# Down projection of a decoder layer: splitting its f operands one tile at a time, with a smaller first chunk

## The chip, the cores and the metric

The kernel runs on 1 core of one Trainium2 chip. The metric is the device time of one execution in microseconds (us); lower is better. Three runs of the kernel before gave 2714.26 us as their median, 2711.56 us as the fastest and 2715.88 us as the slowest.

## The reference

The program is one layer of an autoregressive decoder with 512 positions and a model width of 2048, in float32: a mixer of two attentions, then a gated feed-forward part with a short causal convolution. The change touches only the end of the feed-forward part:

```python
def conv_ffn(h, w_up, w_conv, b_conv, w_down):
    S = h.shape[1]
    u = h @ w_up
    up = jnp.pad(u, ((0, 0), (CONV_W - 1, 0), (0, 0)))
    conv = b_conv
    for j in range(CONV_W):
        conv = conv + w_conv[j] * up[:, j:j + S]
    gate, val = jnp.split(conv, 2, axis=-1)
    return (jax.nn.silu(gate) * val) @ w_down

x = x + gt_f * conv_ffn(h, w_up[l], w_conv[l], b_conv[l], w_down[l])
```

`f = silu(gate) * val` has 5632 rows (channels) of 512 positions, which are 44 row tiles of 128. The down projection multiplies it with `w_down` (5632 x 2048).

## The kernel before

**Precision.** TensorE multiplies in a shortened float32 format. To keep accuracy, each operand is split into a high part (a copy by ScalarE, line 114) and a low part (the rest, a subtraction by VectorE, line 115), and each product is made of three matmuls (lines 1065 to 1067). Weights are split into three pairs of buffers, `whi` and `wlo`; activations are split into slots.

**Seven products for eight.** `seven` works through a list of `Pair`s. A pair is two output tiles of 128 rows, each 512 positions wide. It is computed by a Strassen-like scheme with seven steps instead of eight quarter products. A step has K products of 128x128 weights with 256 positions, so 3K matmuls. The seven steps use seven operand kinds, in the order `r11`, `t3`, `t2`, `r21`, `t1`, `t4`, `r22`. VectorE also combines the raw weight blocks (line 965, four times a pair), and ScalarE and VectorE take each step's result out of PSUM (lines 969 and 975, or 971 and 977 in the up projection). Weights are prepared two steps ahead of their matmuls (`AHEAD = 2`). The raw weight blocks pass through five buffers, loaded on SP's queue at line 952.

**Up projection.** The up pairs have K = 8. When a pair ends, `ffn_out` convolves its two tiles and makes f, and `f_out` stores f and its differences to scratch memory in DRAM (lines 1373 and 1382, GpSimd's queue).

**Down projection.** The 44 row tiles of f don't fit into the on-chip slots as split operands, so they are worked through in four chunks. `DH` is the number of row-tile pairs in each chunk, which is also K for the steps of its pairs: 6, 6, 5 and 5, that is chunks of 12, 12, 10 and 10 row tiles. A chunk has 8 pairs of output tiles, so 56 steps. The first three chunks add their result to `x1` in DRAM with an accumulating DMA from GpSimd's queue (line 1526); the last chunk loads `x1`, adds it (line 1523) and stores the output (line 1524).

**Making the operands of a chunk.** For each kind of a chunk, `load_set` fetches its half tiles of f from scratch into raw slots with one DMA for each half tile on SP's queue (line 1459), the same queue that loads the weights. `split_set` then turns all raw tiles of that kind into high and low tiles: one ScalarE and one VectorE instruction of 128x512 for each raw tile, three raw tiles a set (the third is half filled where K = 5). A set's high and low tiles stay in their slots until the last pair of the chunk has used this kind. There are 81 slots, handed out from a queue: the slot freed longest ago is taken first. A chunk of 3 raw tiles by 7 kinds holds 42 slots when all of it is split; results on their way to DRAM and the raw tiles use slots too.

**When they are made.** `hook` runs after each step and calls `ahead`, which may split one set and load others if enough slots are free. Far from the end of a chunk a set may be split at every fourth step, and no more than four of seven sets; in the last eight steps of a chunk every step may split one. During the up projection the sets of the first chunk are made under the same rule (50 steps before its end at the earliest), but there the two operands of the up projection hold most slots until its last pair.

A scheduler puts all instructions of each engine into one fixed order, by its own estimate of times and by data dependencies. So where an instruction stands in its engine's queue is known from the built program, and an instruction that waits holds up all that stands behind it in that queue.

Of the kernel before, what the change touches and what calls it, by code (L numbers as in the profile page):

```python
# [19 lines left out]
T = 512  # L20
# [11 lines left out]
def trunk_layer_kernel(  # L32
# [15 lines left out]
    HG=2,  # L48
    AFT=(-1,),
    PEU=((2, 5, 8, 11, 14),) * 2 + ((),) * 6,  # L50
    DH=(6, 6, 5, 5),
):
    nc = tc.nc
    V, A, G, PE, SP = nc.vector, nc.scalar, nc.gpsimd, nc.tensor, nc.sync
# [8 lines left out]
    free = deque(range(n_slots))  # L63
    held = {}

    def get(dt=F32):
        i = free.popleft()
        if cur[i] is None or cur[i].dtype != dt:
            cur[i] = pool.tile([P, T], dt, name=f"slot{i}", tag=f"slot{i}")
        held[id(cur[i])] = i  # L70
        return cur[i]

    def getr():
        return get(F32R)

    def put(*ts):
        for t in ts:
            free.append(held.pop(id(t)))
# [9 lines left out]
    def r32(ap):  # L88
        return ap.bitcast(F32)
# [23 lines left out]
    def split(dst_hi, dst_lo, src):  # L113
        A.activation(dst_hi, src, AF.Copy)  # L114
        V.tensor_tensor(dst_lo, src, r32(dst_hi), ALU.subtract)  # L115
# [137 lines left out]
    for ks in (range(0, 7), range(7, 14), range(14, KD)):  # L253
# [4 lines left out]
        for k in ks:  # L258
            t = get()
# [112 lines left out]
    for g in range(-2, 8):  # L372
        if 0 <= g + 1 < 8:
            ada_sum(g + 1)
        todo = len(plan[g]) if g >= 0 else 0
# [4 lines left out]
        if 0 <= g + 1 < 8:  # L380
            ada_cols(g + 1)
            for k in (2 * g + 2, 2 * g + 3):
                hi, lo, t = getr(), getr(), ht[k % 2]
# [138 lines left out]
    for tb in range(1, 4):  # L522
        S = (tb + 1) * P
        qiT = []
        for cb in range(2):
            t = qi[tb, cb]
# [4 lines left out]
            o = (getr(), getr())  # L531
# [60 lines left out]
    for tb in range(4):  # L592
        t = kva[tb]
# [249 lines left out]
    for k, (dh, dl) in enumerate(mq_d):  # L843
        hi, lo = getr(), getr()
# [48 lines left out]
    HT = T // 2  # L893
# [182 lines left out]
    for i in range(KH // 2):  # L1076
        raw = [get() for _ in range(4)]
        ta, tb_ = get(), get()
        for j in range(2):
            k, o = 2 * i + j, slice(j * HT, (j + 1) * HT)  # L1080
# [260 lines left out]
    for k in range(KD):  # L1341
        t = x1T[k]
        hi, lo = getr(), getr()
# [101 lines left out]

    base = [sum(DH[:c]) for c in range(len(DH))]
    ops = [{n: [] for n in KINDS} for _ in DH]
    held_by = [{n: [] for n in KINDS} for _ in DH]
    todo = deque((c, n) for c in range(len(DH)) for n in KINDS)
    coming = deque()  # L1450

    def load_set():
        c, n = todo.popleft()
        ts = []
        for i in range(DH[c]):
            if i % 2 == 0:
                ts.append(get())
            m, o = KEPT[n]
            SP.dma_start(ts[-1][:, (i % 2) * HT:(i % 2 + 1) * HT], f_d[base[c] + i][m][:, o * HT:(o + 1) * HT])
        coming.append((c, n, ts))  # L1460

    def split_set():
        c, n, ts = coming.popleft()
        for i, t in enumerate(ts):
            hi, lo = getr(), getr()
            w = min(T, (DH[c] - 2 * i) * HT)
            split(hi[:, :w], lo[:, :w], t[:, :w])
            put(t)
            held_by[c][n] += [hi, lo]
            ops[c][n] += [(hi[:, o:o + HT], lo[:, o:o + HT]) for o in range(0, w, HT)]  # L1470

    def need(c):
        return (DH[c] + 1) // 2

    made = [0]

    def ahead(left, last):

        c = (coming or todo or [(9,)])[0][0]
        if c > last or left > 50:  # L1480
            return
        n, spare = need(c), 8 if c else 6
        if coming and coming[0][0] <= c and len(free) >= 2 * n + spare and (left <= 8 or left % 4 == 0 and made[0] < 4):
            made[0] = (made[0] + 1) % 7
            split_set()
        while todo and todo[0][0] <= c and len(coming) < (3 if c or len(free) > 15 else 1) and len(free) >= n + spare:
            load_set()


    def up_hook(q, n):  # L1490
        last = q - (n - 7)
        if last == 0:
            for t in h2[:KH]:
                put(*t)
        elif last in (1, 2, 4, 5):
            for t in tsum[{1: 2, 2: 1, 4: 0, 5: 3}[last]]:
                put(*t)
        elif last == 6:
            for t in h2[KH:]:
                put(*t)  # L1500
        ahead(n - q, 0)
# [33 lines left out]
    def hook(q, n):  # L1535
        if q < n_up:
            up_hook(q, n_up)
            return
        c, r = divmod(q - n_up, 56)
        if r >= 49:  # L1540
            put(*held_by[c][KINDS[r - 49]])
        ahead(0 if (coming or todo or [(0,)])[0][0] == c else 56 - r, c + 1)
# [58 lines left out]
```

## Time and profile before

| What | Value |
|---|---|
| median of three runs | 2714.26 us |
| profiled execution, its own time | 2718.77 us |
| span of its profile | 2716.3 us |
| granted TensorE clock, mean over the span | 0.99 |
| PE busy | 2620.4 us (96%) |
| DVE (VectorE) busy | 2184.6 us (80%) |
| ACT (ScalarE) busy | 1285.3 us (47%) |
| POOL (GpSimd) busy | 270.5 us (10%) |
| first load of a down-projection weight | at 2211.0 us |
| DMA issues of f half tiles, line 1459 | 154, the first at 2049.9 us |

PE are the matmuls, PEld the weight loads of TensorE. Rows of the profile name an instruction by its line, engine, operation and tiles: `slot<-slot` at lines 114 and 115 is the split of an f tile, `whi<-raw` and `wlo<-raw` that of a weight block, `x<-slot` the accumulating DMA into `x1`. A shape such as 128x512 is partitions by elements. Idle time is shown as `[2.81 <-DMA x<-slot]`: the engine sat idle for 2.81 us before the instruction, and what came last was the landing of that DMA. SPq and POOLq are the queues on which SP and POOL issue DMAs.

### The profile page before, as it was taken

The numbers are of one execution on the slowest core, as the hardware profiler recorded it, in microseconds if no ns is written. First come the engines' busy times: TensorE is split into PE (matmuls) and PEld (weight loads), VectorE is DVE, ScalarE is ACT, GpSimd is POOL, SyncE is SP. The second block draws the span as 40 slices with busy tenths as digits, with TensorE's granted clock in tenths as the row PEclk, the third lists the DMA queues.
The fourth block names the chain that finished last, engine by engine and source line by source line (L and its number), as shares of the span: only waits on it lengthen the run. The fifth ranks groups of instructions, "written<-read, shape, count | busy, mean of one in ns | idle before, by whom it ended". The sixth has DMA issues, their size and how long they took to land. (4 is left out here: it accounts for less than half of the span.)

```text
span 2716.3 us, 45517 instructions
## 1 busy us (share of the span) xinstructions
PE 2620.4 (96%) x17200; PEld 2351.7 (87%) x17200; DVE 2184.6 (80%) x3669; ACT 1285.3 (47%) x2069; POOL 270.5 (10%) x495
## 2 busy tenths in 40 slices
PE   6999999998999999999999999999999989898999
PEld 5777687778997767788789999999999989898989
DVE  7877966688878667983778989989889897777778
ACT  4333434334444455332545555555555464545554
POOL 1001011110032222110100000000000001011110
PEclk8999899999999999999999999999999999999999
DMA  9943136664585578962333333433433466766574
GB/s 343 341 153 98 34 110 213 197 214 156 190 269 164 161 255 288 323 238 93 132 114 124 134 137 113 147 120 114 148 120 128 140 205 154 187 141 173 137 206 125
DMA packets 236241, 464.33 MB, mean 171 GB/s; under 512 B 24331, under 2 KB 85413, under 8 KB 236021
## 3 DMA queue, kind: packets, MB, share of 16 engines
q1 hardware_dynamic: 199348, 368.79, 42.5%
q0 software_dynamic: 36640, 92.63, 11.7%
q8 instruction: 134, 2.20, 0.3%
q14 instruction: 87, 0.70, 0.1%
q10 hardware_dynamic: 32, 0.01, 0.0%
HBM read 397.11 MB, written 64.23 MB: 170 GB/s over the span
## 5 line engine op out<-in xcount | busy, mean ns | idle before, releaser
L1065 PE MATMUL bank<-slot,whi 128*128 128x256 f32 x3920 | 1109.9, 283 | 49.4 <-ACT slot L969 17.0
L1067 PE MATMUL bank<-slot,wlo 128*128 128x256 f32 x3920 | 1101.6, 282 | 8.3 <-DVE wlo L115 8.2
L1066 PE MATMUL bank<-slot,whi 128*128 128x256 f32 x3920 | 1104.4, 282 | 0.4 <-DVE slot L115 0.4
L1065 PEld LDWEIGHTS bank<-slot,whi 128*128 128x128 f32 x3920 | 743.4, 190 | 62.4 <-ACT slot L969 22.2
L1067 PEld LDWEIGHTS bank<-slot,wlo 128*128 128x128 f32 x3920 | 739.9, 189 | 10.8 <-DVE wlo L115 10.3
L1066 PEld LDWEIGHTS bank<-slot,whi 128*128 128x128 f32 x3920 | 741.7, 189 | 0.8 <-DVE slot L115 0.6
L114 ACT ACTIVATE whi<-raw 128x1024 fp32r<-128x1024 f32 (+2 forms) x458 | 424.6, 928 | 500.1 <-PE bank L1066 385.5
L115 DVE TENSOR_TENSOR wlo<-raw,whi 128x1024 fp32r<-128x1024 f32 (+2 forms) x458 | 482.1, 1056 | 61.7 <-ACT whi L114 59.6
L106 ACT ACTIVATE whi<-raw 128x1024 fp32r<-128x1024 f32 (+4 forms) x182 | 187.3, 1032 | 396.0 <-PE bank L120 201.8
L107 DVE TENSOR_TENSOR wlo<-raw,whi 128x1024 fp32r<-128x1024 f32 (+4 forms) x182 | 215.7, 1186 | 146.4 <-ACT whi L106 146.0
L965 DVE TENSOR_TENSOR raw<-raw,raw 128x1024 f32<-128x1024 f32 (+2 forms) x252 | 264.8, 1051 | 61.8 <-DMA raw<-in_w_down 33.3
L119 PE MATMUL bank<-wlo,slot 128*128 128x512 f32 (+2 forms) x768 | 297.4, 388 | 0.9 <-DVE wlo L107 0.9
L118 PE MATMUL bank<-whi,slot 128*128 128x512 f32 (+2 forms) x768 | 290.1, 391 | 4.7 <-ACT slot L385 4.3
L120 PE MATMUL bank<-whi,slot 128*128 128x512 f32 (+2 forms) x768 | 293.3, 385 | 0.0
L118 PE MATMUL bank<-slot,whi 128*128 128x512 f32 (+1 forms) x656 | 261.2, 405 | 3.3 <-ACT slot L1346 2.3
L119 PE MATMUL bank<-slot,whi 128*128 128x512 f32 (+1 forms) x656 | 263.1, 402 | 0.7 <-DVE slot L687 0.7
L120 PE MATMUL bank<-slot,wlo 128*128 128x512 f32 (+1 forms) x656 | 257.5, 401 | 0.0
L118 PEld LDWEIGHTS bank<-whi,slot 128*128 128x128 f32 x768 | 145.9, 190 | 36.1 <-ACT slot L385 4.3
L723 DVE SCALAR_TENSOR_TENSOR slot<-slot,c_act,slot 128x512 f32<-128x512 f32 x203 | 148.9, 745 | 33.9 <-DMA slot<-in_w_ada 32.8
L119 PEld LDWEIGHTS bank<-wlo,slot 128*128 128x128 f32 x768 | 146.2, 190 | 30.0 <-DVE wlo L107 1.4
L120 PEld LDWEIGHTS bank<-whi,slot 128*128 128x128 f32 x768 | 144.6, 188 | 29.0 <-issue 0.5
L114 ACT ACTIVATE whi<-slot 128x512 fp32r<-128x512 f32 x204 | 127.0, 630 | 79.4 <-PE bank L1066 63.8
(292 smaller groups left out, 3004.6 us busy)
## 6 DMA issues: line engine op xcount, KB each, us to landing
slot<-in_w_ada SPq DMA_DIRECT2D x344, 256.0 KB, 5.7
raw<-in_w_ups SPq DMA_DIRECT2D x126, 512.0 KB, 4.4
raw<-in_w_in SPq DMA_DIRECT2D x50, 512.0 KB, 3.6
raw<-in_w_down SPq DMA_DIRECT2D x64, 384.0 KB, 3.1
raw<-in_w_down SPq DMA_DIRECT2D x64, 320.0 KB, 3.4
slot<-f SPq DMA_DIRECT2D x154, 128.0 KB, 3.3
slot<-in_w_ups SPq DMA_DIRECT2D x68, 256.0 KB, 2.6
f<-slot POOLq DMA_DIRECT2D x66, 256.0 KB, 5.2
```

The lines of the kernel that those rows point to most:

```text
L106: A.activation(hi, raw[:, :w], AF.Copy)
L107: V.tensor_tensor(lo, raw[:, :w], r32(hi), ALU.subtract)
L114: A.activation(dst_hi, src, AF.Copy)
L115: V.tensor_tensor(dst_lo, src, r32(dst_hi), ALU.subtract)
L118: PE.matmul(o, lh, rh, start=first, stop=False)
L119: PE.matmul(o, lh, rl, start=False, stop=False)
L120: PE.matmul(o, ll, rh, start=False, stop=last)
L723: V.scalar_tensor_tensor(acc, ts[i], c_act[:, k:k + 1], acc, op0=ALU.mult, op1=ALU.add)
L965: V.tensor_tensor(part(o, x, y), part(a, x, y), part(b, x, y), op)
L1065: PE.matmul(o, wh[:, ks], rh, start=first and k == 0, stop=False, skip_group_check=True)
L1066: PE.matmul(o, wh[:, ks], rl, start=False, stop=False, skip_group_check=True)
L1067: PE.matmul(o, wl[:, ks], rh, start=False, stop=last, skip_group_check=True)
```

## The change

`split_set` is replaced by `split_tile`, which splits a single raw tile. `ahead` calls it at every third step from 54 steps before the end of a chunk, and at every step in the last eight; the cap of four sets of seven is gone, and it wants fewer free slots (10 instead of 14 with `c` above 0). Loads are still made a whole set at a time. The chunks become 8, 12, 12 and 12 row tiles, so K is 4, 6, 6 and 6, and the weights are packed to match. With even K no raw tile is half filled any more.

```diff
-    DH=(6, 6, 5, 5),
+    DH=(4, 6, 6, 6),
...
-    def split_set():
-        c, n, ts = coming.popleft()
-        for i, t in enumerate(ts):
-            hi, lo = getr(), getr()
-            w = min(T, (DH[c] - 2 * i) * HT)
-            split(hi[:, :w], lo[:, :w], t[:, :w])
-            put(t)
-            held_by[c][n] += [hi, lo]
-            ops[c][n] += [(hi[:, o:o + HT], lo[:, o:o + HT]) for o in range(0, w, HT)]
-
-    def need(c):
-        return (DH[c] + 1) // 2
-
-    made = [0]
+    def split_tile():
+        c, n, ts = coming[0]
+        i = DH[c] // 2 - len(ts)
+        t = ts.pop(0)
+        if not ts:
+            coming.popleft()
+        hi, lo = getr(), getr()
+        split(hi, lo, t)
+        put(t)
+        held_by[c][n] += [hi, lo]
+        ops[c][n] += [(hi[:, o:o + HT], lo[:, o:o + HT]) for o in (0, HT)]
...
-        if c > last or left > 50:
+        if c > last or left > 54:
             return
-        n, spare = need(c), 8 if c else 6
-        if coming and coming[0][0] <= c and len(free) >= 2 * n + spare and (left <= 8 or left % 4 == 0 and made[0] < 4):
-            made[0] = (made[0] + 1) % 7
-            split_set()
-        while todo and todo[0][0] <= c and len(coming) < (3 if c or len(free) > 15 else 1) and len(free) >= n + spare:
+        spare = 8 if c else 6
+        near = left <= 8
+        if coming and len(free) >= 2 + spare and (near or left % 3 == 0):
+            split_tile()
+        while todo and todo[0][0] <= c and len(coming) < (3 if c or len(free) > 15 else 1) \
+                and len(free) >= DH[c] // 2 + spare:
             load_set()
...
-            for n in (6, 6, 5, 5):
+            for n in (4, 6, 6, 6):
```

## The prediction, made before the changed kernel was run

> **What bounds the kernel now.** I read the page first, for the engine that is nearly always busy, and then cut the down projection into its pairs, to see where that engine is not.
>
> ```profile
> span 2716.3 us, 45517 instructions
> PE   6999999998999999999999999999999989898999
> DVE  7877966688878667983778989989889897777778
> ```
>
> PE is the bound. From slice 8 on its digits are 9 but for three dips near the end, each at a change of chunk. Next comes a view by stretches: the steady up projection, a dip in it, the last up pair, then chunk 0 (pairs 0, 1, 2 to 4, 5 to 7), chunk 1 the same, chunk 2 (pairs 0 and 1, 2 to 4, 5 to 7), chunk 3 (pair 0, pairs 1 to 7). Columns: length, busy time with instructions of PE, PEld, DVE, ACT and POOL, granted clock, DMA share, GB/s.
>
> ```profile
> 2020.00:2040.00 20.00, 20.00 (x171) 20.00 (x170) 17.78 (x27) 10.94 (x17) 1.61 (x3) 1.00 0.46 158
> 2100.00:2120.00 20.00, 18.61 (x157) 18.37 (x156) 15.35 (x20) 7.71 (x10) 1.62 (x3) 1.00 0.50 165
> 2196.05:2222.24 26.19, 21.93 (x170) 21.52 (x169) 24.45 (x35) 17.21 (x29) 0.54 (x1) 0.94 0.81 248
> 2222.24:2244.29 22.05, 17.81 (x127) 16.84 (x127) 20.49 (x31) 14.16 (x23) 2.51 (x4) 0.92 0.75 241
> 2244.29:2261.80 17.51, 15.76 (x130) 15.28 (x129) 12.13 (x16) 8.01 (x12) 0.87 (x1) 1.00 0.61 170
> 2261.80:2307.01 45.21, 44.98 (x381) 44.77 (x379) 35.38 (x45) 22.75 (x34) 5.97 (x7) 1.00 0.59 140
> 2307.01:2358.45 51.44, 45.91 (x379) 44.88 (x378) 39.44 (x54) 30.33 (x50) 4.23 (x5) 1.00 0.68 173
> 2358.45:2378.45 20.00, 16.49 (x130) 15.39 (x129) 14.09 (x21) 8.53 (x13) 1.72 (x2) 1.00 0.75 214
> 2378.45:2395.87 17.42, 15.13 (x129) 14.93 (x128) 13.90 (x19) 7.79 (x12) 2.58 (x3) 1.00 0.51 123
> 2395.87:2440.60 44.73, 44.73 (x380) 44.73 (x379) 34.01 (x43) 22.75 (x34) 5.07 (x6) 1.00 0.61 142
> 2440.60:2491.71 51.11, 45.95 (x380) 44.94 (x379) 40.50 (x58) 29.57 (x50) 4.24 (x6) 1.00 0.67 170
> 2491.71:2523.96 32.25, 26.40 (x213) 25.27 (x211) 21.54 (x33) 14.48 (x25) 3.43 (x4) 1.00 0.66 173
> 2523.96:2563.63 39.67, 38.20 (x319) 37.62 (x317) 30.29 (x45) 20.29 (x34) 5.18 (x7) 1.00 0.61 140
> 2563.63:2607.71 44.08, 39.58 (x316) 37.72 (x315) 33.54 (x53) 24.45 (x45) 10.44 (x16) 1.00 0.73 187
> 2607.71:2623.86 16.15, 14.03 (x107) 13.60 (x106) 11.31 (x18) 6.52 (x11) 3.99 (x6) 0.93 0.75 218
> 2623.86:2712.16 88.30, 88.30 (x737) 87.91 (x736) 74.31 (x110) 44.91 (x75) 1.07 (x2) 0.99 0.45 138
> ```
>
> A matmul costs 20.00 / 171 = 0.117 us. A pair has 21 K of them: 19.66 us at K = 8, 14.74 at 6, 12.29 at 5, 9.83 at 4. Length less that is the loss of a stretch: last up pair 6.5; chunk 0 7.3, 2.8, 1.0 and 7.2; chunk 1 5.3, 2.7, 0.5 and 6.9; chunk 2 7.7, 2.8 and 7.2; chunk 3 3.9 and 2.3. With the 1.4 us idle at 2100 that is 65.5 us, all that any rearrangement of the splits could win. The losses stand where f tiles are split; pairs 2 to 4 of chunk 1, with none, lose 0.2 us each.
>
> How a split costs PE time is seen at one stall:
>
> ```profile
> 2379.12 1.72 POOL L1526 DMA_DIRECT2D x<-slot  x2 [16.58 <-DVE slot L975]
> 2382.77 0.85 ACT L114 ACTIVATE whi<-raw 128x768 fp32r<-128x768 f32 x1 [0.87 <-PE bank L1066]
> 2386.43 0.42 ACT L114 ACTIVATE slot<-slot 128x256 fp32r<-128x256 f32 x1 [2.81 <-DMA x<-slot]
> 2386.75 0.46 ACT L969 ACTIVATE slot<-bank,mod 128x256 f32<-128x256 f32 x1
> 2387.26 0.38 PE L1065 MATMUL bank<-slot,whi 128*128 128x256 f32 x1 [2.29 <-ACT slot L969]
> ```
>
> The split writes into a slot whose old content is still on its way to `x1`. ACT stands 2.81 us, the emptying of a PSUM bank queues behind it, and PE waits 2.29 us for that bank. In all, from the last up pair on:
>
> ```profile
> ACT slot L114 <- DMA x<-slot: 11.2, 7, 2.8
> ACT slot L114 <- DMA slot<-f: 7.8, 5, 4.7
> DVE slot L115 <- DMA x<-slot: 16.7, 8, 3.0
> ```
>
> So 15 waits for a landing, 27.9 us, 1.86 us each, on splits that mostly stand alone. The set as such is not what waits.
>
> **The change part by part.** *Counts.* A chunk of K pairs needs 7 sets. Before, 84 splits, 14 of them half filled; after, 77 full ones.
>
> ```profile
> L115 DVE TENSOR_TENSOR slot<-slot,slot 128x512 fp32r<-128x512 f32 x66 | 43.6, 684 | 9.9 <-DMA x<-slot 5.7 <-ACT slot L114 4.0
> L115 DVE TENSOR_TENSOR slot<-slot,slot 128x256 fp32r<-128x256 f32 x14 | 5.7, 421 | 15.4 <-DMA x<-slot 11.0 <-ACT slot L114 4.4
> L115 DVE TENSOR_TENSOR wlo<-raw,whi 128x768 fp32r<-128x768 f32 x112 | 105.8, 953 | 27.1 <-ACT whi L114 26.2
> L975 DVE SCALAR_TENSOR_TENSOR slot<-bank,mod,slot 128x256 f32<-128x256 f32 x96 | 45.9, 478 | 6.5 <-PE bank L1067 6.5
> ```
>
> DVE gains 7 x 0.684 and loses 14 x 0.421: 1.1 us less, hidden under PE, so nothing; uncovered, 1 us. Matmuls, `x1` DMAs (48) and f loads (154) keep their number. The whole question is position. In the built order of the two programs I counted the splits against the weight splits around them. Last up pair, then pairs 0, 1, ... of each chunk:
>
> - before: 16 | 9, 2, 0, 0, 0, 2, 2, 10 | 5, 2, 0, 0, 0, 2, 2, 10 | 5, 2, 0, 0, 0, 2, 2, 8 | none
> - after: 9 | 8, 3, 2, 1, 1, 4, 2, 4 | 3, 1, 2, 1, 1, 1, 1, 10 | 4, 1, 2, 1, 1, 1, 1, 8 | none
>
> The even spread is real only in chunk 0, where 28 slots are held. At the ends of chunks 1 and 2 two chunks of 42 don't fit into 81, so the burst waits for slots as before.
>
> *Up to chunk 0 (last up pair, pairs 0 and 1).* DVE is busy 57.1 of 65.8 us there, and SP's queue is packed:
>
> ```profile
> 2211.02 1.38 SPq L952 DMA_DIRECT2D raw<-in_w_down  x3
> 2212.45 5.88 SPq L1459 DMA_DIRECT2D slot<-f  x7
> 2219.08 0.33 SPq L952 DMA_DIRECT2D raw<-in_w_down  x1
> 2219.45 8.65 SPq L1459 DMA_DIRECT2D slot<-f  x16
> 2228.20 0.54 SPq L952 DMA_DIRECT2D raw<-in_w_down  x1
> ```
>
> An issue takes 8.65 / 16 = 0.54 us, and weights queue behind it. Splits fall from 27 to 20. Issues of f fall from 67 (30 ahead of the first down weight) to 53 (12 ahead of it), but 41 of these, 22 us, now meet 19.7 us of PE work in pairs 0 and 1 instead of 29.5. The loss of 16.6 scales to 12.3 by splits and 13.1 by issues; I take 12.7: 3.9 less. Bounds: 8 (only what DVE lacks) and 17 (nothing won, since steps are shorter).
>
> *Chunk 0, pairs 2 to 7, at K = 4.* No K = 4 step is in the trace. Its DVE work follows from rows: neighbours in DVE's queue start closer together than they last.
>
> ```profile
> 2382.93 0.96 DVE L965 TENSOR_TENSOR raw<-raw,raw 128x768 f32<-128x768 f32 x1
> 2383.81 0.95 DVE L115 TENSOR_TENSOR wlo<-raw,whi 128x768 fp32r<-128x768 f32 x1
> ```
>
> 0.88 us apart at a duration of 0.96, so 0.08 less. Taking the 0.684 of the 512-column row for the 11 weight splits and combinations and 0.478 for the three results taken from PSUM, a pair costs DVE 11 x 0.60 + 3 x 0.40 = 7.8 of 9.83 us, 79%; 14 f splits in six pairs add 1.4 us to each, 94%. Chunk 3, at 84% (74.31 of 88.30), loses 0.33 us a pair; I take that, 2.0 us. Besides, five of the splits write to slots sent to `x1` three or four steps earlier, as in the stall above: 5 x 1.86 = 9.3. Together 11.3 against 8.2: 3.1 more. Bounds: 2 (no wait shows) and 25 (a rival, below).
>
> *Chunk 1.* Pair 0 carries 3 new splits after 4 in the pair before it, instead of 5 after 10: 5.3 x 7 / 15 = 2.5. Pairs 1 to 6 have five places with such a slot: 9.3 and 1.0 of base; pair 7 keeps its burst, a third of 6.9. In all 15.1 against 15.4: 0.3 less. *Chunk 2.* Pair 0 as in chunk 1 before, 5.3; then 10.3 and 2.3: 17.9 against 17.7, 0.2 more. *Chunk 3.* Pair 0 keeps 3.9, seven K = 6 pairs lose 0.2 each: 5.3 against 6.2, 0.9 less. *The dip at 2100*, a set of three, becomes four single tiles: 1.0 less.
>
> Sum: -3.9 + 3.1 - 0.3 + 0.2 - 0.9 - 1.0 = -2.8. The profiled execution took 2718.77, so 2716.0; it lies 4.5 us above the median shown, so 2711.5.
>
> Rule against rows, outside the sum: the landing of `x1` takes
>
> ```profile
> x<-slot POOLq DMA_DIRECT2D x48, 256.0 KB, 4.8
> ```
>
> 4.8 us from issue. The Trainium skill, DMA: Bandwidth & Descriptors, in "Anatomy of one DMA — SWDGE (gpsimd) path", gives 2.0 us plus bytes over 436 GB/s for a DMA from GpSimd, which makes 2.6 us here, an estimate. By that the slots would be free some 2 us earlier, about what a wait lasts, and the splits would cost nothing; the measured 4.8 us decides, and the 15 waits leave that reading no chance.
>
> **The rivals.** *Slower: short steps against a landing that doesn't shorten.* Place: chunk 0. A K = 4 step lasts 1.40 us, a K = 6 step 2.11; a distance of three steps is 2.1 us shorter, so each of the five waits grows from 1.86 to about 4.0 (+10.5), and a raw weight buffer must be refilled in four steps, 5.6 instead of 8.4 us, out of a queue shared with f loads (+3). Time 2711.5 + 13.5 = 2725. It decides once chunk 0 passes 107 us (78.6 + 21 forecast). For: SP's issues of 0.54 us. Against: the scheduler set these slots three and four steps apart where it had mostly two at K = 6.
>
> *Faster: single splits hide.* If slots rest longer because only one tile is taken at a time, half of each x1 wait goes in 15 places: 2711.5 - 15 x 0.93 = 2697.5. For: chunk 0 has free slots. Against: the waits of before fell on single tiles too.
>
> *The spread doesn't come about.* Only the boundary of chunk 0 changes and the rest is as it was: 2711.5 to 2714, within the forecast's own range of 2706 to 2717.
>
> **How the numbers follow.** Forecast 0.40, faster rival 0.27, slower rival 0.33. About 0.2%, 5.4 us, can be told from no change: faster is below 2708.8, slower above 2719.7. Of the forecast 0.05 lies below that line: faster 0.32, same 0.35, slower 0.33. Range 2695 to 2729, both rivals with 3 us beyond them.
>
> **What would show it.** Right: chunk 0 lasts near 100 us with waits of ACT and DVE on `x<-slot`; chunk 1 and 2 keep a loss near 15 to 18 us, and pair 7 its burst; the up-to-down stretch loses 4 us less. Wrong: chunk 0 above 107 or below 92 us, or no `x<-slot` waits in pairs 1 to 6 of chunks 1 and 2.

## The result, and the profile after

The changed kernel took 2729.82 us, the median of 14 runs (2721.45 to 2736.44); the kernel before took 2714.9 us in 14 runs of the same session (2707.31 to 2722.78). The ratio is 1.0054, 95% interval 1.0041 to 1.0067: slower by half a per cent, where 2711.5 was forecast and 2729 was the upper end of the range.

The page of the changed kernel, its span and PE's forty slices with the granted clock:

```profile
span 2733.5 us, 45498 instructions
PE   6999999999999999999999999999999988898999
PEclk8999999999999999999999999999999999999999
```

The span grew by 17.2 us. Before, PE's dips were single slices; now three slices in a row, which hold chunk 0, are at 8. The view by stretches shows it in the same cuts as in the prediction, with the columns as there: the dip at 2100, the last up pair, then chunk 0 (pair 0, pair 1, pairs 2 to 7), chunk 1 (pair 0, 1 to 6, 7), chunk 2 the same, chunk 3 (pair 0, 1 to 7).

```profile
2100.00:2120.00 20.00, 20.00 (x172) 20.00 (x171) 17.57 (x22) 11.11 (x16) 1.63 (x3) 1.00 0.48 158
2193.30:2215.02 21.72, 21.01 (x171) 20.26 (x170) 21.12 (x31) 14.14 (x23) 0.54 (x1) 1.00 0.79 248
2215.02:2232.41 17.39, 13.34 (x86) 12.48 (x85) 14.51 (x26) 11.23 (x21) 0.66 (x2) 0.80 0.71 229
2232.41:2249.86 17.45, 12.91 (x87) 12.51 (x86) 11.10 (x21) 7.94 (x15) 3.24 (x5) 0.80 0.57 144
2249.86:2331.92 82.06, 67.52 (x507) 64.43 (x505) 58.06 (x98) 42.54 (x80) 10.09 (x13) 0.94 0.64 156
2331.92:2350.14 18.22, 15.83 (x129) 15.15 (x127) 13.18 (x18) 8.09 (x13) 1.49 (x2) 1.00 0.81 238
2350.14:2451.29 101.15, 92.29 (x758) 91.27 (x756) 73.69 (x95) 47.68 (x73) 10.96 (x13) 0.98 0.54 133
2451.29:2469.87 18.58, 16.74 (x127) 16.28 (x126) 17.38 (x25) 13.74 (x24) 1.90 (x3) 0.92 0.87 249
2469.87:2488.24 18.37, 16.25 (x129) 15.59 (x129) 10.09 (x13) 8.17 (x13) 0.86 (x1) 0.99 0.83 236
2488.24:2591.20 102.96, 93.81 (x757) 92.37 (x756) 75.36 (x96) 47.80 (x73) 10.89 (x13) 0.97 0.52 131
2591.20:2606.94 15.74, 15.19 (x129) 14.98 (x128) 13.91 (x20) 10.81 (x18) 8.12 (x15) 1.00 0.94 259
2606.94:2624.68 17.74, 15.61 (x130) 15.18 (x128) 13.35 (x17) 7.26 (x11) 2.32 (x4) 1.00 0.72 224
2624.68:2729.33 104.65, 104.65 (x884) 104.44 (x882) 84.78 (x109) 49.95 (x75) 1.12 (x2) 1.00 0.40 132
```

Length less 21 K matmuls of 0.117 us per pair is the loss, worked out as in the prediction:

| stretch | before | forecast | after |
|---|---|---|---|
| last up pair, chunk 0 pairs 0 and 1 | 16.6 | 12.7 | 2.1 + 7.6 + 7.6 = 17.3 |
| chunk 0, pairs 2 to 7 | 8.2 | 11.3 | 82.06 - 58.95 = 23.1 |
| chunk 1 | 15.4 | 15.1 | 137.95 - 117.9 = 20.0 |
| chunk 2 | 17.7 | 17.9 | 137.07 - 117.9 = 19.2 |
| chunk 3 | 6.2 | 5.3 | 122.39 - 117.9 = 4.5 |
| dip at 2100 | 1.4 | 0.4 | 0.0 |
| sum | 65.5 | 62.7 | 84.1 |

The sum rose by 18.6, the span by 17.2; 1.4 us were won elsewhere. Chunk 0 lasts 116.9 us where about 100 was forecast, and PE loses most in the six pairs behind the start. The waits of the splits and of the weight combinations, from the last up pair on (us in all, times, longest):

```profile
ACT slot L114 <- DMA x<-slot: 22.5, 10, 4.2
ACT slot L114 <- DMA slot<-f: 8.1, 8, 2.6
DVE slot L115 <- DMA x<-slot: 8.8, 3, 3.3
DVE raw L965 <- DMA raw<-in_w_down: 21.7, 20, 3.6
```

Waits for the landing of `x1` are 13 instead of 15, but 31.3 us instead of 27.9: 2.4 us each instead of 1.86. In chunk 0 alone there are six, 14.5 us by the same view, where before there were four, 5.7 us; five of the six, 11.0 us, lie in pairs 2 to 7. What one does to PE, in a timeline of chunk 0, pair 1:

```profile
2232.82 1.83 POOL L1524 DMA_DIRECT2D x<-slot  x2
2240.41 0.63 ACT L114 ACTIVATE slot<-slot 128x512 fp32r<-128x512 f32 x1 [3.46 <-DMA x<-slot]
2240.95 0.61 ACT L114 ACTIVATE whi<-raw 128x512 fp32r<-128x512 f32 x1
2243.17 0.58 PE L1065 MATMUL bank<-slot,whi 128*128 128x256 f32 x1 [3.57 <-ACT whi L114]
```

ACT stands 3.46 us before a split whose slot is still on its way to `x1`; the split of the next weights queues behind it; PE gets no weights for 3.57 us. The landing itself takes a little longer than before, 5.4 us in the median against 4.8:

```profile
x<-slot POOLq DMA_DIRECT2D x48, 256.0 KB, 5.4
```

Behind the stall the matmuls are slow for some microseconds. By stretches, with the columns as above: the stall in pair 0, the time behind it, and the time after that.

```profile
2217.85:2221.59 3.74, 0.28 (x3) 0.08 (x1) 3.57 (x6) 3.74 (x9) 0.00 (x0) 0.94 0.84 255
2221.59:2228.04 6.45, 5.85 (x24) 5.27 (x25) 5.60 (x10) 3.89 (x8) 0.00 (x0) 0.51 0.73 227
2228.04:2236.00 7.96, 7.49 (x60) 7.21 (x60) 7.14 (x14) 4.13 (x9) 3.47 (x5) 1.00 0.55 156
```

24 matmuls took 5.85 us, 0.24 each, at a granted clock of 0.51; then 60 took 7.49, 0.125 each, at 1.00. Added up over stretches of 2 us (length times one less the granted clock, from the last up pair on), such spells lose 18.8 us in the changed kernel's trace, 5.1 in that of before. The Trainium skill, TensorE: Matmul & The Clock Gate, in "Part 1: The HAM clock gate (the "warmup" mystery)", says that TensorE falls to half speed after an idle window of about 3.4 us and needs as long to come back. The trace agrees in part: the clock is 0.51 for 6.45 us behind a stall of PE of 3.46 us, but a slow spell also follows a stall of 1.61 us (last section). So the first reading left two accounts of the 18.6 us: longer stalls, or the slow clock behind them. The first two runs ask which half of the change makes the stalls, the next ones what the landings and the weight buffers cost, and the last four ask about the clock.

### The profile page after: what moved, and what is told of

It reads as the page before. It is cut to its first block, busy times and chain, and to the rows that moved or that the text cites. A ratio compares the mean times of both kernels' runs of the same rounds, so it can differ in the third digit from the quotient of the medians.

```text
span 2733.5 us, 45498 instructions
## 1 busy us (share of the span) xinstructions
PE 2626.9 (96%) x17200; PEld 2358.7 (86%) x17200; DVE 2186.4 (80%) x3662; ACT 1285.1 (47%) x2062; POOL 271.3 (10%) x495
## 5 line engine op out<-in xcount | busy, mean ns | idle before, releaser
L723 DVE SCALAR_TENSOR_TENSOR slot<-slot,c_act,slot 128x512 f32<-128x512 f32 x203 | 149.2, 747 | 32.3 <-DMA slot<-in_w_ada 31.3
```

The source lines that it names most:

```text
L723: V.scalar_tensor_tensor(acc, ts[i], c_act[:, k:k + 1], acc, op0=ALU.mult, op1=ALU.add)
```

## The experiments

Every ratio is to the kernel before, run on the same chip, and stands with its 95% interval. A time in us is best compared by its ratio, since the kernel before itself took from 2718 to 2723 us on the chips of these runs.

**Which half of the change.** The chunk sizes alone, with whole sets as before:

```diff
-    DH=(6, 6, 5, 5),
+    DH=(4, 6, 6, 6),
...
-            for n in (6, 6, 5, 5):
+            for n in (4, 6, 6, 6):
```

> The kernel before with the chunk sizes alone changed to 8, 12, 12 and 12; whole sets are still split. Theory A (the steps of the small first chunk, K = 4, are too short for slots that are still being written to x1): slow like the changed kernel, 2724 to 2736 us, chunk 0 above 107 us, waits of ACT and DVE on x<-slot of 1.9 us or more each in chunk 0. Theory B (splitting one tile at a time is what costs, the chunk sizes don't matter): 2710 to 2718 us, chunk 0 below 100 us.

2731.59 us, ratio 1.0043 (1.0029 to 1.0058). The view by stretches over its chunk 0:

```profile
2211.41:2327.39 115.98, 92.10 (x674) 87.54 (x673) 84.01 (x144) 59.45 (x113) 13.64 (x17) 0.91 0.65 168
```

Chunk 0 is as long as in the changed kernel, with a loss of 115.98 - 78.6 = 37.4. So the chunk sizes make it, with whole sets as with single tiles, though the places differ: pair 0 loses 13.6 us here and pairs 2 to 7 lose 18.4.

Tile by tile alone, in the old chunks; two tiles a step in the last eight steps ahead of chunk 0, since its sets are larger:

```diff
+        i = (DH[c] + 1) // 2 - len(ts)
+        w = min(T, (DH[c] - 2 * i) * HT)
...
+        for _ in range(2 if near and c == 0 else 1):
+            if coming and coming[0][0] <= c and len(free) >= 2 + spare and (near or left % 3 == 0):
+                split_tile()
```

> The changed kernel with the old chunks of 12, 12, 10 and 10 row tiles; one tile a step, but two where the first chunk needs them (it has 21 tiles to split now, in place of 14). Theory A: within 5 us of the kernel before, 2710 to 2720 us, since no step is shorter than K = 5. Theory B: slow, 2724 us or more, with waits on x<-slot in more places than before.

2726.67 us, ratio 1.0019 (1.0004 to 1.0034): a small loss, 6.1 us above the kernel before beside it, so just past what Theory A allowed and far from the whole slowdown. Its waits from the last up pair on:

```profile
ACT slot L114 <- DMA x<-slot: 24.6, 10, 4.2
DVE slot L115 <- DMA x<-slot: 13.7, 5, 4.3
```

There are 15, as before, but 38.3 us in all, 2.55 each. A tile taken at every third step meets slots no better rested than a set does.

**Without the landings.** Both kernels with the accumulating DMAs of chunks 0 to 2 left out, so that no slot is ever on its way to `x1`. The outputs lack what these chunks add.

```diff
-                    G.dma_start(x1_d[n], u, accum_op=ALU.add)
+                    pass
```

> The changed kernel without the accumulating DMAs of chunks 0 to 2 into x1 (their results are left out of the output). Theory A: the stalls of chunk 0 go, chunk 0 falls from 117 to 90 us or less, the whole to about 2690 us, and the distance to the kernel before without the same DMAs shrinks below 4 us. Theory C (f loads on SP's queue and the load on VectorE at K = 4 set the pace, the landing of x1 is incidental): chunk 0 stays above 105 us and the whole above 2715 us.

> The kernel before without the accumulating DMAs of chunks 0 to 2 into x1 (their results are left out of the output). Theory A: the 27.9 us of waits on x<-slot go, and most of them come back as time: 2690 to 2697 us. Theory C: 2708 us or more.

The changed kernel falls to 2692.47 us, ratio 0.9897 (0.9875 to 0.9918), the kernel before to 2691.05, 0.9888 (0.9866 to 0.9911). The difference of 15 us between them shrinks to 1.4; the intervals allow about 8 either way. That is Theory A's forecast, except that chunk 0 stays at 101.65 us where 90 or less was expected. Chunk 0 of each, by stretches, the changed kernel first:

```profile
2216.08:2317.73 101.65, 89.09 (x675) 84.45 (x674) 84.08 (x142) 62.15 (x116) 1.62 (x3) 0.97 0.52 156
```

```profile
2214.91:2345.00 130.09, 122.51 (x1009) 120.23 (x1009) 109.71 (x145) 74.95 (x119) 1.62 (x3) 1.00 0.50 154
```

With K = 4 chunk 0 still loses 23.1 us, with K = 6 it loses 12.1 (a trace that lies 7 us below its kernel's median, so somewhat more by the median). The last up pair, 2.2 against 7.1, gives back half of that. So the DMAs into `x1` carry most of the slowdown, but short steps cost something without them too. These runs take away the waits and the traffic of the DMAs together. The built order moves a little when DMAs go, so single stretches here are to be read with care.

**Separate slots for the results.** A kernel can keep the DMAs and still not wait: four slots are set aside for the results of the down pairs, and no split is ever given one of them.

```diff
+    ring, made_u = deque(), [0]
+    def get_u(down):
+        if down and made_u[0] >= 4:
+            return ring.popleft()
+        made_u[0] += bool(down)
+        return get()
...
-                E["u1"] = get()
+                E["u1"] = get_u(p.scale)
...
-            put(*us, *x1)
+            ring.extend(us)
+            put(*x1)
```

> The changed kernel, but the results of the down pairs rotate among four slots of their own, so that no split writes into a slot on its way to x1; the DMAs stay. Theory A (slots still being written to x1): the waits of splits on x<-slot go and the time falls near that without the DMAs, 2692 to 2706 us. Theory D (the DMAs cost by their traffic, which delays f and weight loads): 2720 us or more. Four slots fewer for the splits may cost up to 5 us at the ends of chunks 1 and 2.

> The same four slots in the kernel before. Theory A: 2693 to 2706 us, within 5 us of the changed kernel with the four slots, so that the change is then worth next to nothing either way. Theory D: 2712 us or more.

2715.11 us for the changed kernel, 0.9976 (0.9964 to 0.9987), between the two theories, and 2706.19 for the kernel before, 0.9944 (0.9923 to 0.9965), at the end of Theory A's range. The two lie 8.9 us apart, not within 5: with the splits' waits for `x1` gone from both kernels, but not the DMAs, more than half of the 15 us is still there. No split waits for `x1` in either, and the loss of chunks 1 and 2 of the changed kernel falls from 39.2 to 22.1. But chunk 0 still takes 111.73 us. What DVE waits for there:

```profile
DVE raw L973 <- DMA raw<-in_w_down: 10.1, 9, 2.4
```

The combinations of weights wait for weights that haven't landed, 8.8 us of it in pairs 2 to 7. If short steps are too short for a refill of the raw buffers, then a K = 4 chunk must suffer at the other end too, where no f tile is split.

```diff
-    DH=(6, 6, 5, 5),
+    DH=(6, 6, 6, 4),
...
-            for n in (6, 6, 5, 5):
+            for n in (6, 6, 6, 4):
```

> The kernel before with chunks of 12, 12, 12 and 8 row tiles: the K = 4 steps come last, where no splits of a next chunk are queued between them. If K = 4 steps alone are slow (VectorE and the weight loads at the short step), chunk 3 loses 10 us or more against 6.2 before and the whole is 2722 us or more. If they are slow only with splits among them, chunk 3 loses 7 us or less and the whole is within 6 us of the kernel before.

> Both: four slots for the results, and chunks of 12, 12, 12 and 8. If the two effects add, 2690 to 2704 us.

2738.36 us without the separate slots, 1.0063 (1.0043 to 1.0082), and 2710.24 with them, 0.9959 (0.9944 to 0.9973), where 2690 to 2704 was expected. Chunk 3 of the first by stretches, and its wait for weights there:

```profile
2635.43:2727.12 91.69, 84.87 (x674) 81.79 (x672) 73.35 (x126) 45.78 (x86) 2.90 (x4) 0.98 0.46 134
```

```profile
DVE raw L965 <- DMA raw<-in_w_down: 13.0, 9, 5.7
```

The loss is 91.69 - 78.6 = 13.1 us, where K = 6 in the same place loses 4.5 and K = 5 lost 6.2. With the separate slots it is 88.11 - 78.6 = 9.5. A K = 4 step costs on its own. It is not the whole of the 16 us by which the first run is slower: its chunks 0, 1 and 2 lose 21.2, 22.4 and 20.7 us, against 18.2, 15.4 and 17.7 before.

The cure, if it is the refill: in chunk 0 the weight blocks, 512 columns wide, fit a slot, so they can be loaded into slots and leave the five raw buffers. This is added to the changed kernel with separate result slots.

```diff
             def new(slots=False):
+                if W <= T:
+                    return [(get(), 0, W)]
...
-                if len(t) == 1:
+                if len(t) == 1 and id(t[0][0]) not in held:
```

> The changed kernel with four slots for the results, and in chunk 0 the raw weight blocks (512 columns, the size of a slot) go into free slots instead of the five raw buffers, so that a weight load needn't wait for a raw buffer four steps earlier. Theory A2 (what is left of chunk 0's loss, 33 us, is in pairs 2 to 7 the short refill time of the raw buffers): chunk 0 falls by 6 to 12 us, to 100 to 106 us, the whole to 2703 to 2710 us. Rival E (the splits' own work on ACT and DVE between short steps): chunk 0 stays at 110 us or more.

2704.59 us, 0.9940 (0.9920 to 0.9959). Chunk 0 by stretches:

```profile
2220.20:2323.64 103.44, 87.98 (x675) 84.39 (x673) 83.30 (x142) 61.49 (x116) 13.73 (x17) 0.95 0.71 177
```

103.44 us instead of 111.73, as Theory A2 had it; pairs 2 to 7 lose about 9 us instead of 18. That the five raw buffers cost chunk 0 some 8 us is shown. Waiting for weights has not ended, though: the combinations (now line 975) wait for blocks that land in slots, three times instead of eight in pairs 2 to 7, 5.8 us instead of 8.8.

```profile
DVE slot L975 <- DMA slot<-in_w_down: 5.8, 3, 2.3
```

The 16 us of pairs 0 and 1 stay.

**A version that beats both.** With the separate slots the other choices were tried once more: a reserve of 4 free slots instead of 8 with whole sets and old chunks, the same with tile by tile, and the small first chunk with every aid.

> The kernel before with four slots for the results and with the reserve of free slots lowered from 8 to 4, since the results need none of them any more. If the remaining loss at the ends of chunks is late slots, 2698 to 2705 us; if it is the burst itself, within 3 us of the four slots alone (0.994 of the kernel before).

> One tile per step, old chunks, four slots for the results, reserve of 4. With the waits on x1 gone, splitting tile by tile should cost nothing: within 0.2% of whole sets with the four slots (0.994 of the kernel before). If tile by tile is bad for itself, 0.997 or more.

> The changed kernel (chunks of 8, 12, 12 and 12, one tile a step) with all three aids: four slots for the results, chunk 0's raw weight blocks in slots, reserve of 4. If the small first chunk is worth something once its waits are gone, it beats the old chunks with the same aids (0.9910 of the kernel before): 0.990 or less. If the K = 4 steps still cost, 0.992 to 0.995, with chunk 0 near 100 us.

Sets: 2709.83 us, 0.9959 (0.9944 to 0.9974), no better than separate slots alone. Tiles: 2694.82, 0.9910 (0.9895 to 0.9926), better than the 0.994 that was expected. The small first chunk: 2704.7, 0.9933 (0.9912 to 0.9955). The second is the best of all, some 0.9% below the kernel before. Its chunk 0:

```profile
2223.68:2352.64 128.96, 122.89 (x1010) 120.31 (x1010) 107.67 (x143) 75.28 (x119) 13.69 (x17) 1.00 0.69 179
```

128.96 - 117.9 = 11.0 lost, against 18.2 before, at a full clock. With the same separate slots and the same reserve, single tiles are 15 us faster than whole sets: splitting tile by tile does what it was meant to, once its slots are free of landings. The small first chunk is slower than the old chunks even so (0.9933 against 0.9910).

**The clock.** Do stalls cost what they last, or also the slow matmuls behind them? In the changed kernel useless matmuls were put into the step ahead of each of the six stalls of 3.0 us and more. `warm` is a small constant tile; the fillers are tied behind that step's last matmul, write to a part of PSUM that nothing reads, and take no wait away.

```diff
+        def fillers(mm, q):
+            if q - AHEAD - len(steps) not in FILL:
+                return
+            for _ in range(40):
+                with tc.issue_after(mm.ins), tc.high_priority(offset=2000):
+                    mm = PE.matmul(pairs_of_banks[((q - AHEAD) // 7 + 2) % 4][0][:, HT:HT + P], warm, warm, start=True,
+                                   stop=True, skip_group_check=True)
...
-            ev()
+            ev(); fillers(last_mm, q)
```

> The changed kernel with 40 useless matmuls (128x128 by 128 columns, into a part of PSUM that nothing reads, by estimate 0.06 us each, 2.4 us in all) right behind the last matmul of the step ahead of each of six stalls of PE that lasted 3.0 to 3.7 us: steps 1, 10, 45 and 52 of chunk 0, step 29 of chunks 1 and 2. They add work and take no wait away; what the kernel computes is unchanged. Theory C (the clock): a stall of 3 us or more is followed by some 3.4 us or more at half clock, with matmuls 0.21 instead of 0.117 us apart, 18.8 us of lost clock from the last up pair on in the changed kernel against 5.1 before; with the fillers the stalls fall to about 1 us, the lost clock to 7 us or less, and the time to 2716 to 2721, a ratio to before of 1.000 to 1.003. Theory D (the clock is slow for another reason, or what it loses would be lost in waits anyway): lost clock stays at 15 us or more, or falls while the waits grow by as much; 2728 to 2735.

> The changed kernel unaltered, beside the one with fillers and on the same chip: 1.0054 as before, and lost clock of 15 to 20 us from the last up pair on by both theories; it shows how far two traces of one kernel differ in their stalls.

With 40 at each place 2741.65 us, 1.0067 (1.0055 to 1.0079); the changed kernel again, 2732.49, 1.0038 (1.0026 to 1.0050). PE's groups show why the first can't decide:

```profile
L1057 PE MATMUL bank<-warm 128*128 128x128 f32 x240 | 27.5, 273 | 0.0
```

27.5 / 240 = 0.115 us each: half the columns of the kernel's own matmuls, and no shorter. Forty last longer than a stall. So fewer:

> As with 40 fillers, but 20 at each of the six places: one took 0.115 us, not 0.06, so 40 of them were 4.6 us, longer than the stalls of 3.0 to 3.7 us that they should fill, and added PE work of their own. 20 are 2.3 us and leave 0.7 to 1.4 us of each stall. Theory C (lost clock adds to the time): lost clock from the last up pair on 8 us or less, and the time 4 to 12 us below that of the changed kernel, 2717 to 2726, a ratio to before of 0.999 to 1.001. Theory D (what the clock loses would otherwise be lost in waits, since the chain through ACT, DVE and the landings sets the pace at these places): lost clock 8 us or less too, but the time within 4 us of the changed kernel's, a ratio of 1.003 to 1.006.

> 10 fillers at each of the six places, 1.15 us, so that a stall of 3.4 us leaves 2.3 us of idle time. Theory C: lost clock between 5 and 12 us and a ratio of 1.000 to 1.003. Theory D: 1.003 to 1.006, whatever the lost clock.

Twenty: 2734.0 us, 1.0058 (1.0038 to 1.0077). Ten: 2730.02, 1.0046 (1.0028 to 1.0064). The stalls of 3.0 us and more went from five in the repeat to none with 40 and with 20 and to one with 10. But the slow clock did not go: the lost clock, worked out as above, was 8.7 us with 40, 13.6 with 20, 10.2 with 10, and 11.9 in the repeat of the unaltered kernel (15 to 20 was expected there), since shorter stalls, some of 1.6 to 2.0 us, were followed by slow spells too. And not all fillers stood in a stall. In the run with ten, behind step 45 of chunk 0:

```profile
2306.88 1.23 PE L1057 MATMUL bank<-warm 128*128 128x128 f32 x10
2307.94 0.33 PE L1074 MATMUL bank<-slot,wlo 128*128 128x256 f32 x1
2311.82 0.36 PE L1072 MATMUL bank<-slot,whi 128*128 128x256 f32 x1 [2.49 <-DVE slot L975]
```

PE goes on at once behind the fillers, with ten matmuls of its own, and stalls only then. So it was at three of the six places (steps 10, 45 and 52 of chunk 0) with ten and with 20; there the fillers came ahead of the stall, not in it, and one block of 20 ran at half clock itself and took 4.36 us. By its ratio none of the three kernels is faster than the one without fillers, and the ratios with 20 and with ten lie where Theory D put them; but as the slow clock was not taken away, the runs decide between neither theory.

How much lost clock adds to the time stays open. Two traces of the changed kernel differ by 6.9 us of it (18.8 and 11.9) but by only 2 us in the time from the last up pair on (535.7 and 533.7). Over its 14 and its 12 runs, each microsecond of lost clock (the span times one less the run's granted clock, which is known to 2.7 us) goes with some 0.6 us of time, with correlations of 0.54 and 0.63; as longer stalls bring both, that is no proof.

## Why the prediction was wrong

**Chunk 0, pairs 2 to 7: the step that failed.** Forecast a loss of 11.3, measured 23.1: 11.8 of the 21.4 us by which the sum was off. Of the two terms the waits for `x1`, 5 x 1.86 = 9.3, came out nearly as forecast: there are five in these pairs, 11.0 us. From the view of waits over 2249.86 to 2331.92:

```profile
ACT slot L114 <- DMA x<-slot: 7.7, 4, 4.1
DVE slot L115 <- DMA x<-slot: 3.3, 1, 3.3
DVE raw L965 <- DMA raw<-in_w_down: 6.0, 5, 2.4
```

The term that failed is the base of 2.0 us, what K = 4 steps lose without those waits; it was read from DVE's load in chunk 3 at K = 5. With separate slots no split waits for `x1`, and these pairs still lose 17.8 us; with the weight blocks in slots as well they lose 8.8. So the base was too small by nearly 16 us, and some 9 of them are the refill of the five raw buffers, which the base left out and the slower rival had priced at 3. What makes up the other 7 is not shown. Chunk 3 at K = 4, without a split, lost 13.1 or 9.5. The waits themselves cost less than their length here: without them these pairs lose 5.3 us less, not 9.3.

The slow clock had no term either: new stalls were priced at their own length. By the clock column about 5 us went by at half clock in pairs 2 to 7 and about 7 in pairs 0 and 1; how much of that adds to the time is open, as said.

**Up to chunk 0.** Forecast 3.9 won, measured 0.7 lost: 17.3, just past the bound of 17 that was named "nothing won, since steps are shorter". The counts were right and the last up pair lost only 2.1 instead of 6.5; the loss moved into pairs 0 and 1, 15.2 us instead of 10.1, with one wait for `x1` of 3.46 us in pair 1 that the forecast didn't have. Scaling a loss by the number of splits and issues didn't hold; that the PE work which covers them shrank by a third would explain it, but no run shows it. Pairs 0 and 1 lose 15.9 us with separate result slots and blocks in slots too, and 9.8 with the DMAs to `x1` left out. What part of it is SP's packed queue, what DVE, and what the clock at 0.80 was not taken apart.

**Chunks 1 and 2.** 4.9 and 1.3 us above the forecast. Pairs 1 to 6 of each were to have five waits of 1.86 us; there were three in chunk 1, 9.6 us, and two in chunk 2, 6.6 us. So the waits were fewer and longer: single waits of 4.2 and 3.7 us, where the largest before was 3.0, stop PE for over 3 us, and the pair in which they fall, pair 4, has the largest loss of each chunk (5.6 and 6.3 us). That the three of chunk 1 add up to about the forecast (9.6 against 9.3) is luck. The cause was right: with separate slots the two chunks lose 22.1 together, 17 less than with shared ones.

**Chunk 3 and the dip.** 0.8 and 0.4 us below the forecast: right.

**The rule on landings.** The prediction set 4.8 us against an estimate of 2.6 from the Trainium skill, DMA: Bandwidth & Descriptors, "Anatomy of one DMA — SWDGE (gpsimd) path". The median after is 5.4, and leaving the landings out took the changed kernel from a ratio of 1.0054 to 0.9897: the measured number decides.

**The rivals.** The slower one named the right place, the right sign and two causes at work, and its point of decision, chunk 0 past 107 us, was passed at 116.9. Its sizes were off in opposite ways: five waits that grow to 4.0 us lasted 2.2, and a refill of 3 us was worth some 9. That its 2725 is only 5 us short is luck in part. The faster one falls as put, since waits grew on single tiles too (the run with tiles alone is at 1.0019). The third falls with the table. The chance was misplaced: what the trace had on a K = 4 step, a landing and a refill that don't get shorter with it, spoke for the slower rival. The argument against it, that the scheduler had put the slots three and four steps apart, rested on the built order and on no measured time, and it bore on the waits alone, not on the refill.

**What is shown.** The sizes alone give 0.43% of the 0.54%. Leaving out the DMAs into `x1` shrinks the difference between the kernels from 15 us to 1.4, with about 8 either way; taking away only the splits' waits for them leaves 8.9. So these waits are a part of the cause and not all of it. The rest may come from the traffic of these DMAs: in chunk 0 of the changed kernel DVE waits 10.1 us for raw weights with the DMAs and separate slots, and 5.6 us without the DMAs. That was not tested by itself. The five raw buffers cost chunk 0 some 8 us. How the rest of chunk 0 splits between its first two pairs' causes stays open, and so does the clock's own share.

## What to carry to other kernels

When a loop's step gets shorter, list what behind it has a fixed length (a landing of a stored tile, the refill of a buffer) and cost each in steps; a loss that was read at the longer step leaves them out. A buffer that goes out by DMA should not return to a pool from which latency-bound work draws: four slots set apart were worth 0.56% here, and only then did spreading the splits pay (0.9910). And when work is put into a stall as a test, look in the trace whether it stands there and whether what it was to remove is gone.

## What the runs showed of the hardware

The slow clock goes by windows. In the clock records of the 18 traces every spell of half clock lasts 3.41 us or a multiple of it, but for the last, which the end of the trace cuts, and within a trace all begin on one grid of 3.41 us. Whether a window at full clock is followed by a slow one goes with how long PE was idle in it. Two windows of the changed kernel, each with its successor, columns as above:

```profile
2463.46:2466.87 3.41, 1.57 (x12) 1.16 (x10) 3.41 (x6) 3.03 (x5) 0.00 (x0) 1.00 1.00 345
2466.87:2470.29 3.42, 3.42 (x16) 3.42 (x17) 2.50 (x5) 1.26 (x2) 0.85 (x1) 0.50 0.98 306
2439.57:2442.98 3.41, 1.77 (x15) 1.56 (x14) 1.62 (x3) 1.99 (x4) 0.00 (x0) 1.00 0.51 138
2442.98:2446.40 3.42, 3.42 (x30) 3.42 (x30) 2.76 (x5) 2.20 (x4) 0.00 (x0) 1.00 0.10 19
```

PE was idle for 1.84 us in the first and for 1.64 us in the third; half clock follows the first alone. From 2190 us on, 64 windows at full clock had more than 1.86 us of idle time, and each was followed by one at half clock; of 95 with 1.29 to 1.86 us 14 were, and of 2497 with less none. So it counts how much of a stall falls into one window, about half of it being enough. All 32 stalls of PE of 3.0 us or more were followed by at least 2 us of half clock, with matmuls some 0.21 us apart instead of 0.117; of 40 between 2.0 and 3.0 us 23 were, and a stall of 1.61 us in chunk 1, pair 7 of the changed kernel was as well.

A matmul of 128 columns took 0.115 us back to back, one of 256 columns 0.117, in these f32 forms. Two traces of the same kernel, 2 us apart in span, differed by 6.9 us in time lost at half clock.
